# First FFN loop with shift rows from TensorE, and padded SBUF tiles: one layer of a latent diffusion backbone on Trainium2

## The chip, the core and the metric

The kernel runs on one NeuronCore of a Trainium2 chip. Its metric is the time of one execution in device microseconds (us). Three executions of the kernel before took 1124.28, 1126.04 and 1126.17 us; the median is 1126.04 us. Engines are named as in the profile: PE (TensorE, the matrix multiplier; PEld is its weight load), DVE (VectorE), ACT (ScalarE), POOL (GpSimd) and SP (SyncE, which issues nearly all DMAs here).

## What is computed

All of it is float32. `x` holds 512 latent tokens and `ctx` 256 context tokens, both 1024 wide. The change touches the first sublayer, for both streams:

```
mx = split(silu(c) @ w_ada + b_ada, 9)        # latent: shift, scale, gate, ...
mc = split(silu(c_ctx) @ w_ada + b_ada, 9)    # context
def ffn_sublayer(h_in, shift, scale, gate, norm_w, w1, w3, w2):
    h = rms_norm(h_in, norm_w) * (1 + scale) + shift
    return h_in + 0.5 * gate * swiglu(h, w1, w3, w2)
x   = ffn_sublayer(x,   mx[0], mx[1], mx[2], ...)    # D_FF = 2816
ctx = ffn_sublayer(ctx, mc[0], mc[1], mc[2], ...)
...   # token mixing (attention and gated MLP), then a second FFN, on x alone
```

## The kernel before, in words

Activations lie transposed: 128 features on the partitions, 8 such tiles (index `k`), 768 tokens on the free axis (two groups of 256 latent and 128 context columns). Each float32 product is made of three matmuls on operands that were split into a high part (rounded, type f32r) and a low part (the rest): high by high, high by low, low by high (`mm3`). Split weights lie in `oph`/`opl` tiles of 512 columns from a pool of 5 pairs (`ops`): ACT copies the high part, DVE subtracts for the low part. The FFN's input `h` lies split in `hh`/`hl`, its inner activation in `gh`/`gl`. A weight load takes 128 columns, 512 bytes of a partition.

**The first loop** begins the first FFN while its inputs still arrive. Before any feature tile `k` can be multiplied, the modulation of that tile must be known: a scale and a shift for each of 128 features and for both streams, each a dot product of 1024 elements with `silu(c)` or `silu(c_ctx)`. For the *scale*, PE multiplies the conditioning vectors (`scw`, 32 columns wide, two of them not zero) with the weights in eight small matmuls (`ada_row`, L330), ACT copies the row out (`ada_copy`), and one PE matmul against `sel` turns it into a column (`ada_col`, L340). For the *shift*, DVE multiplies a weight block laid out by output feature with the conditioning vector spread over all partitions (`cb`) and sums along the row: `ada_sum`, one instruction for each `k` and stream, 16 in all, tile `junk` in the profile. ACT then adds the bias (`ada_s`).

With both, `first_x` (DVE, tile `hfull`), `first_h` (ACT, tile `hh`) and `first_l` (DVE, tile `hl`) make tile `k` of `h`; `oph`/`opl` split the first-layer weights of tile `k` (tile `raw`, from `wfirst`). Then `step_mm(k)` (L604) runs twelve PE matmuls on 512 latent tokens, summed over `k` in four PSUM halves, and `first_ctx(k)` (L589) twelve on 256 context tokens. The loop is written out by hand, and its instructions keep their written order on each engine: step `k` opens with the column of tile `k+1` and the row of tile `k+2`, makes `h` of tile `k+1`, and multiplies tile `k`. The context's norm (squares by ACT, sums by DVE and one PE matmul) is made in steps 2 to 4, its `h` in steps 4 to 6, and `first_ctx` runs in pairs in steps 5 and 6 and for tiles 4 to 7 at the end.

After the loop come the rest of the first FFN, the mixing, and the second FFN, which a fast matrix scheme (tiles `t1h`, `b11h` and so on) runs on 256 columns.

Of the kernel before, what the change touches and what calls it, by code (L numbers as in the profile page):

```python
# [9 lines left out]
F32 = mybir.dt.float32  # L10
# [7 lines left out]
P = 128  # L18
# [155 lines left out]
def layer_kernel(ctx: ExitStack, tc: tile.TileContext, xT, wfirst, wst, wada, wuq, wkpe, cols, wrope, vnw, rope, out):  # L174
# [6 lines left out]
    opp = ctx.enter_context(tc.tile_pool(name="ops", bufs=1))  # L181
    st = Stream(nc, raws, opp, OPS, wst)
# [31 lines left out]
    accs = const.tile([P, NK, 2], F32, name="accs")  # L214
# [3 lines left out]
    b1n = const.tile([P, NK], F32, name="b1n")  # L218

# [15 lines left out]
    with right():  # L235
        hpool = hctx.enter_context(tc.tile_pool(name="hpool", bufs=1))
# [13 lines left out]
    scw = sp.tile([P, NK, 32], F32, bufs=1, name="sc")  # L250
    sc = scw[:, :, 0:2]
    sel = sp.tile([P, 2], F32, bufs=1, name="sel")
# [8 lines left out]
    sblk, units, raws_ = [], [], []  # L261

    def first_scale(k):
        ra = sp.tile([P, D], F32, tag="sa", bufs=3, name=f"scale_{k}")
        pin(nc.sync.dma_start(ra, wada[k][:, :D]))
        units.append([ra])

    def first_shift(k):
        if k % 2 == 0:
            pool, tag, bufs = (sp, "sb", 1) if k == 4 else (st.raw_pool, "block", BLOCKS)  # L270
            sblk.append(pool.tile([P, 2048], F32, tag=tag, bufs=bufs, name=f"shift_{k}"))
        rs_ = sblk[-1][:, (k % 2) * D : (k % 2) * D + D]
        pin(nc.sync.dma_start(rs_, wada[k][:, D:]))
        units[k].append(rs_)
# [6 lines left out]
    def first_units(k):  # L281
        first_scale(k)
        first_shift(k)
        first_raw(k)

    for k in range(3):
        first_units(k)
    nc.vector.tensor_reduce(sel, ident.rearrange("p (q c) -> p c q", c=32)[:, 0:2, :], axis=AX.X, op=ALU.add)
# [7 lines left out]
    def ada_dot(raw, c, which, to=None):  # L296
# [3 lines left out]
        nc.vector.scalar_tensor_tensor(  # L300
            out, raw, 1.0, cb[:, which, :], ALU.mult, ALU.mult,
            accum_out=acc[which][:, c : c + 1] if to is None else to,
        )
# [26 lines left out]
    def ada_row(d):  # L330
        for kt in range(NK):
            q = slice(kt % 4 * 32, kt % 4 * 32 + 32)
            pin(nc.tensor.matmul(pa[q, :P], scw[:, kt, :], units[d][0][:, kt * P : kt * P + P], start=kt < 4, stop=kt >= NK - 4))

    def ada_copy(d):
        row = sp.tile([P, P], F32, tag="row", name=f"row_{d}")
        nc.scalar.copy(row, pa[:, :P])
        return row

    def ada_col(row, d):  # L340
        o = pcol[:, 2 * d : 2 * d + 2]
        pin(nc.tensor.matmul(o, row, sel, start=True, stop=True))
        nc.scalar.activation(
            pairs[0][1][:, d, :], o, AF.Identity, bias=b1n[:, d : d + 1], scale=col[:, COL_N1 + d : COL_N1 + d + 1])
# [7 lines left out]
    def ada_shift(d, which):  # L352
        ada_sum(d, which)
        ada_s(d, which)
# [108 lines left out]
    def square1(j):  # L463
        sq = sp.tile([P, 512], F32, tag="sqx0", bufs=4, name=f"sq0_1{j}")
# [7 lines left out]
    def rstd_tiles(which):  # L472
        n = parts[which][1]
        return [sp.tile([P, n], F32, bufs=1, name=f"{s}{which}") for s in ("r0", "v")]
# [52 lines left out]
    put_cb(0)  # L527
    nc.vector.tensor_scalar_add(b1, col[:, COL_B : COL_B + 72], 1.0)
# [3 lines left out]
    def oph(k):  # L532
        ops[k] = st.pair() if k != OPS else [sp.tile([P, 512], F32R, tag="sqx0", bufs=4, name=f"op5{p}") for p in "hl"]
# [20 lines left out]
    put_cb(1)  # L554
    oph(0)
    steps(0)
    ada_row(0)
    row = ada_copy(0)
    late_sums(1)
    ada_col(row, 0)  # L560
    ada_sum(0, 0)
    ada_s(0, 0)
    root(1)
# [3 lines left out]
    first_units(3)  # L567
    ada_row(1)
    row = ada_copy(1)
    first_l(0, 0, 0)  # L570
    oph(1)
    steps(1)
    first_x(0, 0, 1)
    opl(1)
    first_h(0, 0, 1)
    first_units(4)
    load_x(0, 4, slice(256, 384))
# [35 lines left out]
    def step_open(k):  # L613
        ada_col(row, k + 1)
        if k + 2 < NK:
            ada_row(k + 2)

    sqs = []
    first_half(0)
    ada_col(row, 1)  # L620
    first_l(0, 0, 1)
    ada_row(2)
    row = ada_copy(2)
    ada_sum(1, 0)
    ada_s(1, 0)
    first_half(1)
    first_x(1, 0)
    first_h(1, 0)
    ada_sum(2, 0)
    first_l(1, 0)  # L630
    oph(2)
    opl(2)
    ada_s(2, 0)
    first_scale(5)
    load_x(4, 4, slice(256, 384))
    first_shift(5)
    first_raw(5)

    step_open(1)
    first_x(2, 0)  # L640
    first_h(2, 0)
    row = ada_copy(3)
    ada_sum(0, 1)
    first_l(2, 0)
    ada_sum(3, 0)
    oph(3)
    opl(3)
    ada_s(3, 0)
    ada_s(0, 1)
    step_mm(1)  # L650

    step_open(2)
    first_x(3, 0)
    first_h(3, 0)
    row = ada_copy(4)
    ada_sum(1, 1)
    oph(4)
    for j in (0, 1):
        sqs.append(square1(j))
    first_l(3, 0)  # L660
    ada_sum(4, 0)
    opl(4)
    ada_s(1, 1)
    ada_s(4, 0)
    step_mm(2)
    for k in (6, 7):
        first_scale(k)
        first_raw(k)
    for k in (6, 7):
        first_shift(k)  # L670

    step_open(3)
    first_x(4, 0)
    first_h(4, 0)
    for j in (2, 3):
        sqs.append(square1(j))
    row = ada_copy(5)
    ada_sum(5, 0)
    first_l(4, 0)
    ctx_add(2, 0)  # L680
    ctx_add(3, 1)
    ada_s(5, 0)
    oph(5)
    opl(5)
    ctx_add(2, 3)
    nc.vector.tensor_add(sqs[2][:, 0:256], sqs[2][:, 0:256], sqs[2][:, 256:512])
    step_mm(3)

    step_open(4)
    first_mm(4, 0)  # L690
    sumc = mm()
    sums(sumc, sqs[2][:, 0:256], True, True)
    first_mm(4, 1)
    first_x(5, 0)
    first_h(5, 0)
    row = ada_copy(6)
    first_l(5, 0)
    ada_sum(6, 0)
    ada_s(6, 0)
    rc = rstd_tiles(1)  # L700
# [4 lines left out]
    for j in (0, 1):  # L705
        first_x(j, 1)
        first_h(j, 1)
    ada_sum(2, 1)
    for j in (0, 1):
        first_l(j, 1)  # L710

    pcs += [mm() for _ in range(NFIRST)]
    step_open(5)
    first_x(6, 0)
    first_h(6, 0)
    row = ada_copy(7)
    ada_sum(3, 1)
    for j in (2, 3):
        ada_s(j, 1)
    first_l(6, 0)  # L720
    for j in (2, 3):
        first_x(j, 1)
        first_h(j, 1)
    ada_sum(7, 0)
    for j in (2, 3):
        first_l(j, 1)
    step_mm(5)
    for j in (0, 1):
        first_ctx(j)
    ada_s(7, 0)  # L730
    oph(6)
    opl(6)

    step_open(6)
    first_x(7, 0)
    first_h(7, 0)
    ada_sum(4, 1)
    first_l(7, 0)
    for j in (2, 3):
        first_ctx(j)  # L740
    oph(7)
    opl(7)
    ada_sum(5, 1)
    for j in (4, 5):
        ada_s(j, 1)
        first_x(j, 1)
        first_h(j, 1)
    ada_sum(6, 1)
    for j in (4, 5):
        first_l(j, 1)  # L750
    ada_sum(7, 1)
    for j in (6, 7):
        ada_s(j, 1)
        first_x(j, 1)
        first_h(j, 1)
    for j in (6, 7):
        first_l(j, 1)
    step_mm(6)

    step_mm(7)  # L760
    for j in range(4, NK):
        first_ctx(j)
# [1476 lines left out]
```

## Time and profile before

| | |
|---|---|
| median of three runs | 1126.04 us |
| the profiled execution | 1126.13 us |
| its span in the trace | 1124.3 us |
| PE busy | 1109.6 us, 99% of the span |
| DVE / ACT / POOL busy | 906.1 / 540.1 / 311.4 us |
| granted PE clock, mean | 0.998 |
| first loop, from the span's start to the first matmul of the next stage | 67.10 us |

Times in the trace count from the span's start; about 1.8 us of an execution lie outside the span. A matmul's recorded duration contains its pipeline's length, so that the records of neighbours overlap and busy PE time says little about its pace. The pace is the distance from one start to the next. A window of the trace counts every matmul that touches it, so (window + one recorded duration) / count gives that distance.

### The profile page before, as it was taken

To read this page: it belongs to the slowest core of one execution; us is meant where nothing else is said; L and a number is where in the kernel's file an instruction comes from. 1 tells how busy PE (TensorE), PEld (TensorE's weight loads), DVE (VectorE), ACT (ScalarE), POOL (GpSimd) and SP (SyncE) were. 2 spreads that over 40 slices of the span, in tenths; PEclk is the share of its full clock that TensorE was granted. 3 is DMA by queue.
4 is the path that set the end of the run, shared out by engine and by line. 5 is a ranking of instruction groups with operands and counts; after the bars stand their busy time and mean duration, and the time that the engine had idled before them with its cause. 6 is when DMAs were issued, how large, how long until landed. Compare 5 with 4: busy or idle time off the path is not lost.

```text
span 1124.3 us, 18769 instructions
## 1 busy us (share of the span) xinstructions
PE 1109.6 (99%) x7078; PEld 1060.7 (94%) x7078; DVE 906.1 (81%) x1669; ACT 540.1 (48%) x1119; POOL 311.4 (28%) x268
## 2 busy tenths in 40 slices
PE   8799999999999999999999999999999999999998
PEld 6699999999999999999998889999989989898997
DVE  7989999888888778866855899978886969686884
ACT  5555422441344213444755559985553535353451
POOL 0002402420343013300008427750014425162330
PEclk9999999999999999999999999999999999999999
DMA  9630253244234664322233211003221422233302
GB/s 350 215 113 20 102 194 121 96 164 151 94 131 150 230 207 167 129 66 87 85 131 93 76 38 35 25 20 116 73 95 57 148 79 84 105 113 113 114 1 94
DMA packets 35674, 125.89 MB, mean 112 GB/s; under 512 B 3712, under 2 KB 10624, under 8 KB 30976
## 3 DMA queue, kind: packets, MB, share of 16 engines
q1 hardware_dynamic: 35440, 124.63, 32.8%
q8 instruction: 56, 0.92, 0.3%
q14 instruction: 34, 0.28, 0.1%
q10 hardware_dynamic: 144, 0.06, 0.0%
HBM read 122.58 MB, written 2.10 MB: 111 GB/s over the span
## 4 chain that ended last, share of the span: by engine, by line
PE 91%; DVE 6%; ACT 1%; issue 1%; DMA 0%; POOL 0%; SPq 0%; DVEq 0%; POOLq 0%; ACTq 0%
PE mm L59 57%; PE one L59 20%; PE big L59 8%; PE mm L168 2%; PE mm L169 2%; PE mm L170 2%; DVE junk L59 1%; PE mm L589 1%; DVE opl L59 1%; DVE hfB L59 1%; DVE hfull L59 1%; DVE hl L59 1%; PE big L604 1%; DMA x<-xT 0%; DVE v L59 0%
## 5 line engine op out<-in xcount | busy, mean ns | idle before, releaser
L59 DVE TENSOR_TENSOR opl<-block,oph 128x512 fp32r<-128x512 f32 x216 | 192.3, 897 | 29.7 <-ACT oph L59 26.9
L59 POOL TENSOR_TENSOR block<-block 128x512 f32<-128x512 f32 x69 | 104.9, 1521 | 391.1 <-DVE opl L59 388.4
L59 ACT CAST oph<-block 128x512 fp32r<-128x512 f32 x216 | 133.8, 621 | 111.9 <-PE mm L59 85.1
L59 PE MATMUL mm<-gh,oph 128*128 128x384 f32 (+1 forms) x440 | 155.4, 353 | 0.0
L59 PE MATMUL mm<-gh,opl 128*128 128x384 f32 (+1 forms) x440 | 155.0, 352 | 0.0
L59 PE MATMUL mm<-gl,oph 128*128 128x384 f32 (+1 forms) x440 | 154.9, 352 | 0.0
L59 DVE SCALAR_TENSOR_TENSOR x<-mm,g,x 128x256 f32<-128x256 f32 (+2 forms) x184 | 84.6, 498 | 48.5 <-PE mm L59 48.2
L59 ACT CAST oph<-raw 128x512 fp32r<-128x512 f32 x115 | 69.9, 620 | 78.6 <-PE mm L59 53.1
L59 PEld LDWEIGHTS mm<-gh,opl 128*128 128x128 f32 x440 | 82.6, 188 | 5.7
L59 PEld LDWEIGHTS mm<-gl,oph 128*128 128x128 f32 x440 | 82.6, 188 | 5.6
L59 PEld LDWEIGHTS mm<-gh,oph 128*128 128x128 f32 x440 | 82.6, 188 | 5.6
L59 POOL TENSOR_TENSOR block<-s,block 128x512 f32<-128x512 f32 x35 | 48.0, 1371 | 143.7 <-DVE opl L59 143.1
L59 DVE TENSOR_TENSOR opl<-raw,oph 128x512 fp32r<-128x512 f32 x115 | 77.4, 688 | 7.2 <-ACT oph L59 6.5
L59 PE MATMUL mm<-hh,oph 128*128 128x384 f32 x192 | 64.9, 338 | 0.0
L59 PE MATMUL mm<-hh,opl 128*128 128x384 f32 x192 | 64.5, 336 | 0.0
L59 PE MATMUL mm<-hl,oph 128*128 128x384 f32 x192 | 64.5, 336 | 0.0
L59 DVE SCALAR_TENSOR_TENSOR junk<-raw,cb 128x1024 bf16<-128x1024 f32 x48 | 62.2, 1309 | 0.3 <-DMA raw<-wada 0.3
L59 POOL TENSOR_TENSOR s<-block 128x512 f32<-128x512 f32 x34 | 55.6, 1634 | 9.9 <-DMA block<-wst 9.9
L59 PE MATMUL one<-hh,opl 128*128 128x384 f32 x144 | 48.4, 336 | 0.0
L59 PE MATMUL one<-hh,oph 128*128 128x384 f32 x144 | 48.4, 336 | 0.0
L59 PE MATMUL one<-hl,oph 128*128 128x384 f32 x144 | 48.4, 336 | 0.0
L59 DVE SCALAR_TENSOR_TENSOR raw<-raw,cb 128x1024 f32<-128x1024 f32 x32 | 41.0, 1289 | 8.1 <-DMA raw<-wada 8.1
(685 smaller groups left out, 3403.0 us busy)
## 6 DMA issues: line engine op xcount, KB each, us to landing
raw<-wst SPq DMA_DIRECT2D x77, 512.0 KB, 3.9
block<-wst SPq DMA_DIRECT2D x36, 1024.0 KB, 4.9
raw<-wada SPq DMA_DIRECT2D x56, 512.0 KB, 4.3
scale<-wada SPq DMA_DIRECT2D x8, 512.0 KB, 8.4
shift<-wada SPq DMA_DIRECT2D x8, 512.0 KB, 8.9
x<-xT SPq DMA_DIRECT2D x5, 512.0 KB, 6.3
raw<-wfirst SPq DMA_DIRECT2D x8, 256.0 KB, 7.6
out<-x SPq DMA_DIRECT2D x7, 256.0 KB, 2.2
```

What stands on the lines that cost most here:

```text
L59: return lambda *a, **k: self.tc.keep_in_program_order(f(*a, **k))
L168: nc.tensor.matmul(out, lh, rh, start=first, stop=False, skip_group_check=more)
L169: nc.tensor.matmul(out, lh, rl, start=False, stop=False, skip_group_check=more)
L170: nc.tensor.matmul(out, ll, rh, start=False, stop=last, skip_group_check=more)
L589: pin(nc.tensor.matmul(o, l[:, c], r, start=k == 0 and m == 0 and w == 0, stop=k == NK - 1 and m == 2, skip_group_check=True))
L604: pin(nc.tensor.matmul(two(pbs[i]), l[:, c], lat(r, k), start=False, stop=k == NK - 1 and m == 2, skip_group_check=True))
```

## The change

**The first loop.** The shift's weights are laid out like the scale's, and PE makes both: `ada_row` runs 16 small matmuls in place of 8, the second eight with the conditioning vectors two columns further right in `scw` (now 34 columns wide), so that shift lands in its own two rows. `sel` has four columns, `ada_col` makes four values, and ACT finishes scale and shift with one instruction each. The 16 DVE dots, their 16 `ada_s` and the accumulators `accs` go. Scale and shift of a tile lie in one 1 MB tile (`scale_k`); four such tiles exist, two in the pool `block` and two in the pool `start`. All context work moves to the end: its columns of `x` are loaded after the last weights of `w_ada`, squares and sums stand in steps 5 and 6, and all eight `first_ctx` run behind `step_mm(7)`. The split weights of tiles 5, 6 and 7 lie in the pool `start`.

```diff
+    scw = sp.tile([P, NK, 34], F32, bufs=1, name="sc")
+    sc = scw[:, :, 2:4]
...
     def ada_row(d):
-        for kt in range(NK):
-            q = slice(kt % 4 * 32, kt % 4 * 32 + 32)
-            pin(nc.tensor.matmul(pa[q, :P], scw[:, kt, :], units[d][0][:, kt * P : kt * P + P], start=kt < 4, stop=kt >= NK - 4))
+        for w in range(2):
+            for kt in range(NK):
+                q = slice(kt % 4 * 32, kt % 4 * 32 + 32)
+                pin(nc.tensor.matmul(pa[q, :P], scw[:, kt, 2 - 2 * w : 34 - 2 * w], units[d][w][:, kt * P : kt * P + P],
+                                     start=w == 0 and kt < 4, stop=w == 1 and kt >= NK - 4))
...
     def ada_col(row, d):
...
+        nc.scalar.activation(pairs[0][0][:, d, :], o[:, 2:4], AF.Identity, bias=col[:, d : d + 1])
-    def ada_sum(d, which):
-        ada_dot(units[d][1], d, which, accs[:, d, which : which + 1])
-    def ada_s(d, which):
-        nc.scalar.activation(mod_s[0][which][:, d : d + 1], accs[:, d, which : which + 1], AF.Identity, bias=col[:, d : d + 1])
...
     step_mm(7)
-    for j in range(4, NK):
+    ctx_h((4, 5))
+    ctx_h((6, 7))
+    for j in range(NK):
         first_ctx(j)
```

On DVE, steps 3 and 4 of the loop before read as follows (`hfull`, `hl`: parts of `h`; `junk`: a shift's dot; `opl`, `op5l`: a low part of split weights; `sq`: the context's sum of squares):

```order
L59 SCALAR_TENSOR_TENSOR hfull<-x,a_79,v_214 128x2x256
L59 SCALAR_TENSOR_TENSOR junk_468,accs<-shift_279,cb 128x1024
L59 SCALAR_TENSOR_TENSOR hl<-hfull,s_78,hh 128x2x256
L59 TENSOR_TENSOR sq_12_461<-sq_12_461,sq_10_413 128x512
L59 TENSOR_TENSOR sq_13_463<-sq_13_463,sq_11_415 128x512
L59 TENSOR_TENSOR op5l<-raw_348,op5h 128x512
L59 TENSOR_TENSOR sq_12_461<-sq_12_461,sq_13_463 128x512
L59 TENSOR_TENSOR sq_12_461<-sq_12_461 128x256
L59 SCALAR_TENSOR_TENSOR hfull<-x,a_79,v_214 128x2x256
L59 SCALAR_TENSOR_TENSOR hl<-hfull,s_78,hh 128x2x256
L59 SCALAR_TENSOR_TENSOR junk_523,accs<-shift_446,cb 128x1024
```

And on DVE in the change, from step 4 to the context's norm:

```order
L59 SCALAR_TENSOR_TENSOR hfull<-x,a_83,v_224 128x2x256
L59 SCALAR_TENSOR_TENSOR hl<-hfull,s_82,hh 128x2x256
L59 TENSOR_TENSOR op6l<-raw_416,op6h 128x512
L59 SCALAR_TENSOR_TENSOR hfull<-x,a_83,v_224 128x2x256
L59 SCALAR_TENSOR_TENSOR hl<-hfull,s_82,hh 128x2x256
L59 TENSOR_TENSOR op7l<-raw_451,op7h 128x512
L59 TENSOR_TENSOR sq_11_575<-sq_11_575,sq_10_573 128x512
L59 TENSOR_TENSOR sq_12_577<-sq_12_577,sq_11_575 128x512
L59 TENSOR_TENSOR sq_13_579<-sq_13_579,sq_12_577 128x512
L59 TENSOR_TENSOR sq_13_579<-sq_13_579 128x256
L59 SCALAR_TENSOR_TENSOR hfull<-x,a_83,v_224 128x2x256
```

The dots are gone from between the parts of `h`, and the sums of squares stand behind the split of tile 7's weights, ahead of the last latent `hfull`.

On SP, the end of the loop's loads before (`scale`, `shift`: `w_ada`; `raw` from `wfirst`: first-layer weights; `x` in 128x8x128: context columns; `wst`: weights of the next stage):

```order
L258 DMA x_71<-xT 128x8x128
L265 DMA scale_5_343<-wada 128x1024
L258 DMA x_71<-xT 128x8x128
L273 DMA shift_4_279<-wada 128x1024
L278 DMA raw_347_348<-wfirst 128x512
L265 DMA scale_6_436<-wada 128x1024
L278 DMA raw_438_439<-wfirst 128x512
L265 DMA scale_7_441<-wada 128x1024
L278 DMA raw_443_444<-wfirst 128x512
L273 DMA shift_6_446<-wada 128x1024 x2
```

And in the change:

```order
L270 DMA scale_6_358<-wada 128x1024 x2
L274 DMA raw_367_368<-wfirst 128x512
L270 DMA scale_7_405<-wada 128x1024 x2
L274 DMA raw_415_416<-wfirst 128x512
L260 DMA x_75<-xT 128x8x128 x2
L127 DMA block_794_795<-wst 128x2048
L274 DMA raw_450_451<-wfirst 128x512
```

The context columns moved behind the last `scale` tile, and the last first-layer weights (`raw_450_451`, of tile 7) stand behind a 1 MB block of the next stage. Behind the loop the five engines' instructions stand in the same order as before.

**The padding.** Three unused tiles of 224, 256 and 32 bytes (per partition) shift what is allocated after them; `accs` (64 bytes) is gone.

```diff
+    ctx.enter_context(tc.tile_pool(name="pad2", bufs=1)).tile([P, 64], F32, name="pad_mid")
...
-    accs = const.tile([P, NK, 2], F32, name="accs")
...
+    const.tile([P, 56], F32, name="pad_left")
...
+        ctx.enter_context(tc.tile_pool(name="pad", bufs=1)).tile([P, 8], F32, name="pad_right")
```

The split weights move up by 224 - 64 = 160 bytes, the left side's tiles behind them (`gh`, `gl`) by 416, and the right side's tiles (`hh`, `hl`, and the second FFN's `t` and most `b` tiles, which grow downwards) go down by 32. In the built programs the tiles start at these bytes modulo 512: split weights at 416 before and 64 after, `gh`/`gl` at 416 and 320, `hh`/`hl` and the `t` tiles at 480 and 448. Slices of these tiles begin at multiples of 512 bytes, so a matmul's distance (start of the weights that are loaded under it less start of its moving operand, modulo 512) is the same for all slices. The counts below are of the built program's matmuls that stand beside one of the same width.

| columns | moving operand, weights | matmuls | distance before | after |
|---|---|---|---|---|
| 384 | `h` or its combinations `u`, split weights | 1750 | 448 | 128 |
| 384 | `g`, split weights | 983 | 0 | 256 |
| 512 | `g` or mixed heads, split weights | 601 | 0 | 256 |
| 512 | split weights, `h` as weights | 180 | 64 | 384 |
| 256 | `t`, `b` or `h`, split weights | 1832 | 448 | 128 |

The other f32r matmuls (attention, some 580 at distance 0 among them) keep their distance or are few.

More of the change, by code (lines that the diff above doesn't have):

```diff
@@ L279, in first_raw @@
         raws_.append(rw[:, :W1])
[L281 to L288, printed above, removed]
+    for k in range(4):
+        first_rows(k)
+        if k < 3:
+            first_raw(k)
+    nc.vector.tensor_reduce(sel, ident.rearrange("p (q c) -> p c q", c=32)[:, 0:4, :], axis=AX.X, op=ALU.add)
     warm = mm()
@@ L301, in ada_dot @@
             out, raw, 1.0, cb[:, which, :], ALU.mult, ALU.mult,
[L302 removed]
+            accum_out=acc[which][:, c : c + 1],
         )
@@ L473, in rstd_tiles @@
         n = parts[which][1]
-        return [sp.tile([P, n], F32, bufs=1, name=f"{s}{which}") for s in ("r0", "v")]
+        return [sp.tile([P, n], F32, bufs=1, name=f"{s}{which}") for s in (("v",) if which else ("r0", "v"))]
     def rstd_root(pt, r0):
@@ L566, in layer_kernel @@
     opl(0)
-    first_units(3)
-    ada_row(1)
+    root(1)
     row = ada_copy(1)
     first_l(0, 0, 0)
[L571 to L577, printed above, removed]
+    first_raw(3)
+    first_rows(4)
+    first_rows(5)
     pbs = bigs(4)
@@ L613, in step_open, with next_h @@
     def step_open(k):
-        ada_col(row, k + 1)
+        if k + 1 < NK:
+            ada_col(row, k + 1)
         if k + 2 < NK:
             ada_row(k + 2)
+    def next_h(k):
+        first_x(k, 0)
+        first_h(k, 0)
     sqs = []
     first_half(0)
+    oph(1)
     ada_col(row, 1)
+    steps(1)
+    first_x(0, 0, 1)
+    first_h(0, 0, 1)
+    next_h(1)
     first_l(0, 0, 1)
+    opl(1)
+    first_half(1)
     ada_row(2)
     row = ada_copy(2)
-    ada_sum(1, 0)
-    ada_s(1, 0)
-    first_half(1)
@@ L677, in layer_kernel @@
[L677 to L690, printed above, removed]
-    sumc = mm()
[L692 to L700, printed above, removed]
+    first_raw(6)
@@ new lines, in layer_kernel @@
+    for k in (0, 4):
+        load_x(k, 4, slice(256, 384))
+    for k in range(2, 5):
+        step_open(k)
+        next_h(k + 1)
+        row = ada_copy(k + 2)
+        first_l(k + 1, 0)
+        oph(k + 2)
+        opl(k + 2)
+        if k == 2:
+            first_raw(7)
+        step_mm(k)
+    step_open(5)
+    next_h(6)
+    row = ada_copy(7)
+    first_l(6, 0)
+    oph(7)
+    opl(7)
+    for j in range(4):
+        sqs.append(square1(j))
+    for a, b in ((1, 0), (2, 1), (3, 2)):
+        ctx_add(a, b)
```

161 lines of the change are left out of this document (43 added, 118 removed).

## The prediction

> **What bounds the kernel now.** First the page: busy time, and the chain of work that ended last.
>
> ```profile
> PE 1109.6 (99%) x7078; PEld 1060.7 (94%) x7078; DVE 906.1 (81%) x1669; ACT 540.1 (48%) x1119; POOL 311.4 (28%) x268
> PE 91%; DVE 6%; ACT 1%; issue 1%; DMA 0%; POOL 0%; SPq 0%; DVEq 0%; POOLq 0%; ACTq 0%
> ```
>
> PE holds 91% of the chain, DVE 6%. So two things can move the time: what keeps PE waiting in DVE's 6%, and the pace of the matmuls everywhere else. The change touches both, and I take them apart. The windows of the first loop and the end of its chain say where the 6% lies:
>
> ```profile
> core 0: us, PE busy (x) PEld busy (x) DVE busy (x) ACT busy (x) POOL busy (x), PEclk, DMA share, GB/s
> 0.00:16.50 16.50, 13.16 (x91) 10.39 (x91) 8.70 (x22) 10.89 (x22) 0.69 (x6) 1.00 0.92 326
> 16.50:40.00 23.50, 19.99 (x163) 15.17 (x164) 22.29 (x39) 12.60 (x33) 0.00 (x0) 1.00 1.03 374
> 40.00:51.40 11.40, 7.85 (x59) 6.22 (x58) 10.57 (x22) 5.94 (x15) 0.00 (x0) 1.00 0.20 58
> ...
> 55.72 5.70 PE big L604 x24
> 61.42 5.68 PE mm L589 x48
> 67.10 4.16 PE mm L59 x24
> ```
>
> DVE is busy 22.3 of 23.5 us and then 10.6 of 11.4, while PE has gaps; the loads are over at about 40 us (58 GB/s after it). From 51.4 us on PE runs without a wait and reaches the next stage at 67.10. DVE sets this loop, and after 40 us nothing else does.
>
> **The loop, step by step.** What goes from DVE is one row:
>
> ```profile
> L59 DVE SCALAR_TENSOR_TENSOR junk<-shift,cb x16: 1216/1218/1221, 14.1 to 59.4; 128x1024 bf16<-128x1024 f32 x16
> ```
>
> 16 x 1.22 us and their reads of the accumulator, some 20 us. DVE stops being the bound here, and the question is what is late next: PE's own work, or the loads. PE's work has these prices:
>
> ```profile
> 16.47 0.74 PE L596 MATMUL big<-hh,oph 128*128 128x256 f32 x4 [1.06 <-ACT hh L59]
> ...
> 20.41 0.63 PE L596 MATMUL big<-hh,opl 128*128 128x256 f32 x4
> ...
> 40.28 0.28 PE L342 MATMUL mm<-sel,row 128*128 128x2 f32 x2
> 40.49 0.65 PE L333 MATMUL mm<-scale,sc 128*32 128x128 f32 x16
> 41.06 0.73 PE L604 MATMUL big<-hh,op5h 128*128 128x512 f32 x2
> ```
>
> A column takes 0.21 us (40.28 to 40.49), a row 0.57 (to 41.06). The second eight matmuls follow with the pipeline full, so I price a double row at twice that less one start, 1.02 us; its bounds are 0.57 (all hidden) and 1.14. A step's twelve matmuls take 5.70 / 2 = 2.85 us, a context tile's 5.68 / 4 = 1.42. Both halves of tile 0 end at about 20.8 us (20.41 plus four matmuls); the steps ahead of that need the same loads and the same short DVE work, less one dot, plus a longer row while PE waits, so I leave 20.8. From there PE owes six double rows (6.1), six columns (1.3), seven steps (20.0), the context's sum (0.4) and eight context tiles (11.4): 39.2 us, and without a wait the next stage starts at **60.0 us**.
>
> The loads: 326 GB/s over 16.5 us and 374 over 23.5 is 14.2 MB by 40 us. In the order of the change, tile 7's first-layer weights come behind 2.1 MB of `x`, 8.4 of `w_ada`, 2.1 of `wfirst`, 1.0 of context columns and a 1.0 MB block of the next stage: 14.7 MB, so at 41.5 us. The wait is new: ACT's `oph` of tile 7 waits for it, and queued behind on ACT are the four squares and the last `hh`; behind these on DVE the sums of squares and the last `hfull`; PE's sum of the context, in the middle of step 6, waits for both. Rows of the loop before price them:
>
> ```profile
> 30.48 1.15 ACT L59 ACTIVATE sq<-x 128x512 f32<-128x512 f32 x2
> ...
> 37.17 0.68 DVE L59 TENSOR_TENSOR sq<-sq,sq 128x512 f32<-128x512 f32 x1
> 37.89 0.43 DVE L59 TENSOR_TENSOR sq<-sq 128x256 f32<-128x256 f32 x1
> ...
> 43.76 0.88 DVE L59 SCALAR_TENSOR_TENSOR hfull<-x,a,v 128x256 f32<-128x256 f32 x2
> ```
>
> The split of tile 7 takes 0.6 us, the squares 4 x 0.58, DVE's last two adds 1.1: the sum is ready at about 45.6. PE would reach it at 43.9. I add 1.7 us for that, 0.3 for tile 7's `h`, and 0.5 for short waits on ACT: **62.5 us**, or 4.6 us less than 67.10. The context's `h` (on DVE 16 x 0.44 us from 49 us on) stays ahead of its matmuls, 1.42 us a tile. The bounds: no wait, -7.1 us; or a longer wait that also costs the clock, as here after the gaps up to 51.4 us:
>
> ```profile
> 52.57 0.38 PE L589 MATMUL mm<-hl,oph 128*128 128x256 f32 x1
> ...
> 55.30 0.41 PE L589 MATMUL mm<-hh,opl 128*128 128x256 f32 x1
> ```
>
> 14 rows, so 13 spacings of 210 ns where 113 to 118 is usual: some 1.3 us lost, and that with 2 us more of waiting gives -1. Elsewhere DVE's relief is worth nothing, PE bounding.
>
> **The distances.** The loop is 6% of the time; the matmuls' pace is the rest. It is read from the first and last row of a stretch without a gap. In pairs: 384 columns at distance 448 (117 rows) and at 0 (118 rows), 256 columns at 448 (189) and at 0 (94), 512 columns at 0 (94) and at 64 (70).
>
> ```profile
> 83.75 0.34 PE L59 MATMUL big<-hl,oph 128*128 128x384 f32 x1
> ...
> 103.86 0.34 PE L59 MATMUL mm<-u2h,oph 128*128 128x384 f32 x1
> ...
> 149.69 0.33 PE L59 MATMUL mm<-gh,oph 128*128 128x384 f32 x1
> ...
> 169.97 0.33 PE L59 MATMUL mm<-gh,oph 128*128 128x384 f32 x1
> ...
> 857.79 0.28 PE L59 MATMUL one<-b21h,oph 128*128 128x256 f32 x1
> ...
> 879.93 0.28 PE L59 MATMUL one<-t2h,opl 128*128 128x256 f32 x1
> ...
> 754.78 0.28 PE L59 MATMUL mm<-mixh,uo1l 128*128 128x256 f32 x1
> ...
> 765.95 0.28 PE L59 MATMUL mm<-mixh,uo0l 128*128 128x256 f32 x1
> ...
> 895.84 0.39 PE L59 MATMUL mm<-gl,oph 128*128 128x512 f32 x1
> ...
> 916.94 0.39 PE L59 MATMUL mm<-gl,oph 128*128 128x512 f32 x1
> ...
> 612.88 0.40 PE L168 MATMUL mm<-oph,hh 128*128 128x512 f32 x1
> ...
> 628.99 0.40 PE L168 MATMUL mm<-oph,hh 128*128 128x512 f32 x1
> ```
>
> That gives 173.4 and 173.3 ns (20.11 / 116, 20.28 / 117); 117.8 and 120.1 (22.14 / 188, 11.17 / 93); 226.9 and 233.5 (21.10 / 93, 16.11 / 69). At distance 0, 128 more columns cost 53.2 and 53.6 ns, 0.417 a column, so pure streaming would be 106.8, 160.1 and 213.5 ns, and 13.3 ns of each matmul are something else. It does depend on the distance, but not in one direction: 448 is better than 0 at 256 columns and equal at 384; 64 is worse than 0 at 512. Nor on the distance alone:
>
> ```profile
> 46.46 0.28 PE L589 MATMUL mm<-hh,opl 128*128 128x256 f32 x1
> ...
> 48.84 0.28 PE L589 MATMUL mm<-hh,opl 128*128 128x256 f32 x1
> ...
> 64.11 0.28 PE L589 MATMUL mm<-hh,oph 128*128 128x256 f32 x1
> ...
> 65.64 0.28 PE L589 MATMUL mm<-hl,oph 128*128 128x256 f32 x1
> ```
>
> The same code at the same distance 448 runs at 113.3 ns (2.38 / 21) and then at 117.7 (1.53 / 13). The only rows of 384 columns at the distances 128 and 384 are those with `kpw` as weights, though its load is half as wide:
>
> ```profile
> L59 PE MATMUL mm<-hh,opl 128*128 128x384 f32 x192 | 64.5, 336 | 0.0
> L59 PE MATMUL mm<-hh,kpw 128*64 128x384 f32 x16 | 5.3, 332 | 0.0
> ```
>
> The recorded duration, 4 ns shorter, is the nearest row there is to the new distances. Class by class of the table in the section on the change:
>
> 384 columns, 2733 matmuls, to 128 and 256: between -4 ns (`kpw`) and +6.6 (what 64 costs against 0 at 512 columns). I take -2, half of `kpw`'s, for its load is half: **-5.5 us**; ends -10.9 and +18.0.
>
> 256 columns, 1832, to 128: between 113.3 and 120.1, so -4.5 and +2.3 ns. I take -2, between the two paces that one distance already shows: **-3.7 us**; ends -8.2 and +4.2.
>
> 512 columns, 601, from 0 to 256: between 0 and +6.6; I take +3, **+1.8 us**. And 180 from 64 to 384: between -6.6 and 0; I take -2, **-0.4 us**.
>
> Together -7.8 us. The Trainium skill speaks against all of it: "SBUF — State Buffer", section "Who interferes with whom", says that PE and ACT never wait on anyone, and "TensorE: Matmul & The Clock Gate", section on what happens when a matmul is issued, that loading the next weights takes no read bandwidth from the running matmul. By that rule the term is 0; the 117.8 against 120.1 ns above already disagree, though mildly. The latter page's section on the back-to-back gap gives N/2.4 + 2.5 ns, 162.5 at 384 columns; by it the most that distances could give, an estimate, would be some 50 us.
>
> **The sum.** 1126.13 (the profiled execution; 0.09 above the median) - 4.6 - 7.8 = 1113.7, so **1114 us**.
>
> **Rivals.** (a) *The distances do nothing*: matmul starts are set inside PE, and the small differences in the rows belong to their stages. For it: 448 and 0 are alike at 384 columns, and one distance shows two paces. Against: 120.1 at 0 beside 117.8 at 448, each over some 90 matmuls or more. Time: 1126.1 - 4.6 = 1121.5. That the loads eat the loop's gain as well (-1) is the same case's edge, 1125. (b) *The other 13 ns mostly go*: the weight load's reads meet the moving operand's and were at a bad distance everywhere. The best excess seen, 6.5 ns (113.3 - 106.8), for all: -6.8 x 2733 - 4.5 x 1832 - 6.9 x 601 = -31 us, so 1126.1 - 4.6 - 31 = 1090. (c) *The new distances are worse*: 384 columns at 128 and 256 behave as 512 columns do at 64, +6.6 ns. The price is +18 us at `hh` and `gh`, with 256 and 512 columns near zero: 1126.1 - 4.6 + 18 = 1139.5. It decides from +1.7 ns a matmul on (4.6 us / 2733), a quarter of the difference that 64 and 0 show. For it: 0 is the best distance on record at 512 columns, and 601 matmuls leave it.
>
> **How the numbers follow.** Forecast (1104 to 1119) 0.42; (a) 0.18, of which 0.04 is its edge; (b) or more 0.15; (c) 0.25, of which 0.03 stays within the bound. A measurement of this kernel tells about 0.2%, 2.3 us, from no change. Faster 0.42 + 0.14 + 0.15 = 0.71, same 0.04 + 0.03 = 0.07, slower 0.22. The range takes (a), most of (c) and (b) up to near its price: 1092 to 1136, with about 0.1 left out at each end.
>
> **What would show it.** The loop: no `junk` before the next stage, that stage starting at 60 to 64 us, and one PE wait of about 2 us for the context's sum; a start near 66 means that the loads or the clock took it. The distances: starts at 384 columns 171 ns apart, not 173.4; 256 columns 115 to 116; 512 columns near 230. 173.4 in both `hh` and `gh` is (a), under 168 is (b), over 175 is (c). The forecast is wrong if the classes move in opposite directions, for I took one mechanism for all, or if DVE, at 81%, becomes late once PE is faster.

## The result and the profile after

The changed kernel takes **1133.82 us** (median of four executions, 1132.93 to 1133.90) beside 1125.84 for the kernel before (four executions, 1124.28 to 1126.17): ratio 1.0076, 95% interval 1.0064 to 1.0088. It is 8 us slower; 12 us faster was forecast. The profiled execution took 1133.9 us, its span 1132.0, at a mean granted clock of 0.997. The page's busy times, and the engines' shares of the chain that ended last:

```profile
PE 1122.5 (99%) x7206; PEld 1074.6 (95%) x7206; DVE 889.6 (79%) x1637; ACT 537.7 (48%) x1111; POOL 307.8 (27%) x268
PE 95%; DMA 2%; ACT 1%; DVE 1%; issue 0%; POOL 0%; SPq 0%; DVEq 0%; POOLq 0%; ACTq 0%
```

DVE went from 6% of the chain to 1%, as the change meant it to. PE went from 91% to 95% and the loads (DMA) from 0% to 2%: most of what DVE gave up, PE took. Where in time it went is told by the point at which the next stage starts, in the chain's last steps of the first loop (start, duration, engine, tile, line):

```profile
47.26 1.19 PE mm L456 x2
...
54.92 11.44 PE mm L569 x96
66.36 4.22 PE mm L59 x24
```

The next stage starts at 66.36 us in place of 67.10. The loop has won 0.74 us, and the rest of the span has become longer: 1132.0 - 66.36 = 1065.6 against 1124.3 - 67.10 = 1057.2, **8.4 us**. From there on the engines' instructions stand in the same order in both kernels, PE bounding. So the pace is to be read, from first and last rows of stretches of PE's timeline in which no matmul waits. In pairs: 384 columns from `h` and `u`, at distance 128 (116 rows); 384 from `g`, at 256 (117); 256 columns, at 128 (169); 512 from `g`, at 256 (79).

```profile
84.67 0.34 PE L59 MATMUL big<-hh,oph 128*128 128x384 f32 x1
...
104.91 0.34 PE L59 MATMUL mm<-u3l,oph 128*128 128x384 f32 x1
...
149.74 0.33 PE L59 MATMUL mm<-gl,oph 128*128 128x384 f32 x1
...
169.85 0.33 PE L59 MATMUL mm<-gh,oph 128*128 128x384 f32 x1
...
869.78 0.28 PE L59 MATMUL one<-b22h,opl 128*128 128x256 f32 x1
...
889.94 0.28 PE L59 MATMUL one<-b22h,opl 128*128 128x256 f32 x1
...
904.76 0.39 PE L59 MATMUL mm<-gh,opl 128*128 128x512 f32 x1
...
922.44 0.39 PE L59 MATMUL mm<-gh,opl 128*128 128x512 f32 x1
```

That is 20.24 / 115 = **176.0 ns** where it was 173.4; 20.11 / 116 = 173.4 as before; 20.16 / 168 = **120.0** where it was 117.8; 17.68 / 78 = 226.7 as before (226.9). The recorded durations (0.34, 0.28 us to two digits) hardly show it. Two classes lost, and they are the two whose distance went from 448 to 128; the two that went from 0 to 256 stayed, and so did the small one that went from 64 to 384. Over all gapless stretches of the trace the means are 176.0 against 173.3 ns and 119.7 against 117.5: 2.7 x 1750 + 2.2 x 1832 = 8.8 us, the 8.4 us that the rest of the span lost.

The loop's 0.74 us in place of 4.6 has two further causes, both to be seen on the timelines. On ACT and DVE (`op7h`: the split of tile 7's weights; `sq`: the context's squares and sums; behind a row in brackets, how long the engine stood and what ended that):

```profile
42.66 0.62 ACT L59 CAST op7h<-raw 128x512 fp32r<-128x512 f32 x1 [2.06 <-DMA raw<-wfirst]
43.19 2.19 ACT L59 ACTIVATE sq<-x 128x512 f32<-128x512 f32 x4
44.37 2.28 DVE L59 TENSOR_TENSOR sq<-sq,sq 128x512 f32<-128x512 f32 x3 [0.36 <-ACT sq L59]
```

On PE, two 512-column matmuls to a row from 49.10 us on:

```profile
47.26 1.19 PE L456 MATMUL mm<-sq,ones 128*128 128x256 f32 x2 [3.23 <-DVE sq L59]
...
49.10 1.05 PE L584 MATMUL big<-hh,op6l 128*128 128x512 f32 x2
49.95 1.05 PE L584 MATMUL big<-hl,op6h 128*128 128x512 f32 x2
...
53.36 0.63 PE L584 MATMUL big<-hh,op7h 128*128 128x512 f32 x2
53.83 0.62 PE L584 MATMUL big<-hh,op7l 128*128 128x512 f32 x2
...
54.76 0.28 PE L569 MATMUL mm<-hh,oph 128*128 128x256 f32 x1
```

PE stands 3.23 us before the context's sum, which waits for the squares, which wait behind `op7h` for tile 7's weights, as the prediction had it. After that gap PE runs at half its pace: two matmuls take 0.85 us (49.10 to 49.95) until 53.36, then 0.47. The granted clock says the same (third number from the end of each row; columns as in the windows of the prediction):

```profile
40.00:51.40 11.40, 8.18 (x29) 6.33 (x28) 7.28 (x13) 6.51 (x14) 0.00 (x0) 0.79 0.66 259
46.50:53.40 6.90, 6.14 (x15) 4.84 (x16) 5.73 (x13) 3.85 (x7) 0.00 (x0) 0.51 0.13 52
51.40:67.10 15.70, 15.70 (x114) 14.95 (x113) 13.36 (x27) 8.66 (x19) 0.00 (x0) 0.94 0.22 66
```

### The profile page after: what moved, and what is told of

Same layout as the page of the kernel before. It is cut to its first block, busy times and chain, and to the rows that moved or that the text cites. A ratio compares the mean times of both kernels' runs of the same rounds, so it can differ in the third digit from the quotient of the medians.

```text
span 1132.0 us, 18985 instructions
## 1 busy us (share of the span) xinstructions
PE 1122.5 (99%) x7206; PEld 1074.6 (95%) x7206; DVE 889.6 (79%) x1637; ACT 537.7 (48%) x1111; POOL 307.8 (27%) x268
## 4 chain that ended last, share of the span: by engine, by line
PE 95%; DMA 2%; ACT 1%; DVE 1%; issue 0%; POOL 0%; SPq 0%; DVEq 0%; POOLq 0%; ACTq 0%
PE mm L59 56%; PE one L59 20%; PE big L59 8%; PE mm L168 2%; PE mm L169 2%; PE mm L170 2%; PE big L584 1%; PE mm L569 1%; DMA scale<-wada 1%; DMA raw<-wfirst 1%; PE big L170 1%; PE big L168 1%; PE big L169 1%; PE mm L327 1%; DMA x<-xT 0%
```

## The experiments

The theory after the result: the new distances cost 8.4 us in the two classes that went from 448 to 128, and the loop's own gain was eaten by the late load and the half clock. The rivals: the absolute place of the tiles matters, not the distance; or the loop's rewriting itself slows the later stages. Fifteen kernels were run, all timed beside the kernel before on the same chip. "Base" below is the kernel of which only the shown lines are changed.

### One half of the change at a time

loop_only is the changed kernel with the tiles of the kernel before in their places:

```diff
-    ctx.enter_context(tc.tile_pool(name="pad2", bufs=1)).tile([P, 64], F32, name="pad_mid")
...
-    const.tile([P, 56], F32, name="pad_left")
+    const.tile([P, 16], F32, name="pad_left")
...
-        ctx.enter_context(tc.tile_pool(name="pad", bufs=1)).tile([P, 8], F32, name="pad_right")
```

> The change's loop with every tile at the start it had before (split weights and g at 416, h at 480 modulo 512). Theory: the loop gives 0.7 us (next stage at 66.4 us in place of 67.1) and the distances cost the rest, so 1125.2, with starts 173.3 ns apart at 384 columns and 117.8 at 256. Rival: the loop itself puts the later stages into another rhythm; then 176.0 and 120.0 ns stay, and the time stays near 1134.

pads_only is the kernel before, with the three pads of the change (`pad_left` 40 floats, since `accs` is still there):

```diff
+    ctx.enter_context(tc.tile_pool(name="pad2", bufs=1)).tile([P, 64], F32, name="pad_mid")
...
+    const.tile([P, 40], F32, name="pad_left")
...
+        ctx.enter_context(tc.tile_pool(name="pad", bufs=1)).tile([P, 8], F32, name="pad_right")
```

> The loop of before with the change's starts (64, 320 and 448). Theory: 176.0 ns at 384 columns for h and u (1750 matmuls, +4.7 us), 173.3 for g, 120.0 at 256 columns (1832, +4.0 us), so 1134 to 1135. Rival (the loop made the rhythm): 173.3 and 117.8, and 1126.

Measured, beside 1124.54 us for the kernel before on this chip (15 executions): **pads_only 1132.84** (five, 1132.79 to 1134.73), ratio 1.0078, 95% interval 1.0066 to 1.0091; **loop_only 1124.46** (eleven, 1122.85 to 1125.59), ratio 0.9997, 0.9988 to 1.0006. The pads alone make the whole loss, and the loop alone gains nothing that could be measured. The pads' stretches of 384 (115 rows) and 256 columns (169 rows), with the old loop ahead of them:

```profile
84.81 0.34 PE L59 MATMUL big<-hh,opl 128*128 128x384 f32 x1
...
104.87 0.34 PE L59 MATMUL mm<-u3h,opl 128*128 128x384 f32 x1
...
869.74 0.28 PE L59 MATMUL mm<-t1l,oph 128*128 128x256 f32 x1
...
889.90 0.28 PE L59 MATMUL mm<-t1l,oph 128*128 128x256 f32 x1
```

20.06 / 114 = 176.0 and 20.16 / 168 = 120.0, the numbers of the changed kernel. In loop_only, on the other hand, PE's timeline and the chain's end read:

```profile
43.42 0.62 PE L582 MATMUL big<-hl,op6h 128*128 128x512 f32 x2
47.33 0.67 PE L454 MATMUL mm<-sq,ones 128*128 128x256 f32 x2 [3.29 <-DVE sq L59]
...
51.97 0.28 PE L567 MATMUL mm<-hh,oph 128*128 128x256 f32 x1
...
63.89 4.16 PE mm L59 x24
```

The same wait of 3.29 us, but in this execution no half clock: from the sum to the first context tile 4.64 us (47.33 to 51.97) against 7.50 in the changed kernel (47.26 to 54.76), and the next stage at 63.89. So the half clock cost the changed kernel's profile 2.9 us. It does not follow every such wait: loop_only's execution with this profile had a granted clock of 1.0 and took 1123.24 us, another at 1.0 took 1122.85, and the nine others, at 0.997 or 0.998, took 1124.26 to 1125.59.

### The late load

loop_raw7 has loop_only as its base; tile 7's weights get a tile of their own and are issued ahead of the context's columns and of the next stage's block.

```diff
-        rw = st.raw()
+        rw = gp.tile([P, W1], F32, tag="s1", bufs=4, name="raw7") if k == NK - 1 else st.raw()
...
     first_raw(6)
+    first_raw(7)
     for k in (0, 4):
...
-        if k == 2:
-            first_raw(7)
```

> As the first, but tile 7's first-layer weights have a tile of their own and are loaded ahead of the context columns and of the next stage's block. Theory: the wait of 6.8 us for that load and the half clock after it are what ate the loop's gain; without them the next stage starts at 60 to 62 us and the time is 1119 to 1121. Rival: PE's own added work or the context's chain is the bound; then the next stage starts at 65 us or later and the time is 1124 or more.

**1121.04 us** (five, 1120.72 to 1121.27), ratio to the kernel before 0.9967, 0.9954 to 0.9979; the granted clock was 1.0 in all executions. From the PE timeline and the chain:

```profile
45.40 0.67 PE L454 MATMUL mm<-sq,ones 128*128 128x256 f32 x2 [1.08 <-DVE sq L59]
...
61.96 4.16 PE mm L59 x24
```

The wait is 1.08 us in place of 3.29, the half clock is gone, and the next stage starts at 61.96, 5.1 us earlier than in the kernel before. The medians differ by 3.5 us only, because the execution of the kernel before that was profiled was one of its longer ones (1126.13 us, median 1124.54 here); the two profiled executions differ by 1126.13 - 1121.27 = 4.9 us. So the late load, with the half clock behind it, was what kept the loop's gain back. It is the base of what follows.

### Distance or place

shift_all is the kernel before with all three groups of tiles moved, and the distances kept (448 and 0): `pad_left` of 40 and `pad_right` of 88 floats, no `pad_mid`, so that the split weights and `g` start at 64 and `h`, `t` at 128 modulo 512.

> The kernel before with all three kinds of tiles at other starts (64, 64 and 128) but the distances of before (448 and 0). Theory (distance decides): 173.3 and 117.8 ns as before, 1126. Rival (a start's own place decides, a multiple of 64 where before it was 32 past one): 176 and 120 ns, 1134.

1124.32 us (one execution; the kernel before 1124.54). 172 gapless rows of 256 columns:

```profile
863.75 0.28 PE L59 MATMUL one<-b22h,oph 128*128 128x256 f32 x1
...
883.89 0.28 PE L59 MATMUL mm<-t1h,oph 128*128 128x256 f32 x1
```

20.14 / 171 = 117.8, as before the change. The place alone does nothing. dist_0_128 gives the two classes each other's distances, `h` and `t` 0 and `g` 128, and the next three put both at one distance:

```diff
+    ctx.enter_context(tc.tile_pool(name="pad2", bufs=1)).tile([P, 96], F32, name="pad_mid")
...
-    const.tile([P, 16], F32, name="pad_left")
+    const.tile([P, 32], F32, name="pad_left")
```

(`pad_mid` / `pad_left` in floats: dist_0_128 96 / 32, as shown; dist_64_64 112 / 48; dist_192_192 80 / 80; dist_320_320 48 / 112; below, dist_64_0 none / 48; dist_32_32 120 / 40; dist_480_480 8 / 24.)

> The last loop (early load for tile 7) with h at distance 0 and g at 128, the other way round than in the change. Theory (the distance decides, whatever the tile): g's 384 columns at 176.0 ns and h's at 173.3; h's 256 columns at 120.0; so 1121 + 2.7 x 0.98 + 2.5 x 1.8 = 1128. Rival (128 hurts only h, by something else in h's stages): g stays at 173.3.

> The same loop, h and g both at distance 64. Theory: each distance has a pace of its own for each width. Few rows show 64: 113 to 118 ns at 256 columns, 233 at 512; nothing at 384. If 64 mirrors 448 (the cost depends on how far apart the starts are, not on which is ahead), 173.3 and 117.5 ns, 1121. Rival (it depends on which is ahead): 64 lies towards 128, so 175 to 176 ns at 384 columns, some 1126 to 1128.

> h and g both at 192. Nothing on record is nearer than 128 (176.0 and 119.7 ns) and 256 (173.4 and 119.2). If the cost is a hump around 128, between them: 174 to 175 ns, 1124 to 1127. If 128 is the side of a larger hump, over 176 ns and over 1130.

> h and g both at 320. A few rows of attention at 256 columns show 113 to 118 ns there. If 256 to 448 is one flat stretch at 384 columns, 173.3 ns and 116 to 119 at 256 columns, 1120 to 1123. If some distance frees the matmul of the 13 ns, it is here or at 384: then below 170 ns and below 1112.

One execution each: 1129.33, 1124.32, 1122.06 and 1124.06 us (the kernel before on that chip, one execution: 1125.84). In dist_0_128 it is `g` that runs slowly at 384 columns (115 rows):

```profile
149.80 0.34 PE L59 MATMUL mm<-gh,oph 128*128 128x384 f32 x1
...
169.86 0.34 PE L59 MATMUL mm<-gh,oph 128*128 128x384 f32 x1
```

20.06 / 114 = 176.0, while `h` at 0 has 173.3. What is slow at 128 is whatever lies at 128. The other three fit none of their expectations: at 384 columns 64 gives 174.6 ns, between the two values that were expected; 192 gives 173.3, with nothing left of a hump around 128; and 320 gives 174.6, neither 173.3 nor below 170. The table gives the median of gapless groups of twelve matmuls (lowest to highest in brackets where they differ by over 3 ns), of these traces and of those before and after the change:

| distance | 256 columns | 384 columns | 512 columns, `g` moving | 512 columns, split weights moving |
|---|---|---|---|---|
| 0 | 120.0 | 173.3 | 226.7 (to 230.3) | 226.7 |
| 64 | 113.3 (to 117.8) | 174.6 | 233.3 | 233.3 |
| 128 | 120.0 | 175.8 | 232.5 | - |
| 192 | 117.8 (from 113.3) | 173.3 | 228.9 | 228.9 |
| 256 | 120.0 | 173.3 | 226.7 (to 230.3) | - |
| 320 | 113.3 (to 117.8) | 174.6 | 233.3 | 233.3 |
| 384 | - | - | - | 233.3 |
| 448 | 117.8 (from 113.3) | 173.3 | - | 228.9 |

The pattern repeats every 256 bytes (0 and 256, 64 and 320, 192 and 448 agree in every column that has both), and what is best at one width is not at another: 64 is the best distance for 256 columns and the worst for 512.

### Best distance, and the theory's fall

If the distance sets the spacing, then 64 for the second FFN's 256 columns, and nothing else moved (but `b12`, from 0 to 320), should win. ffn2_64 does that on the base loop_raw7:

```diff
+        hactx.enter_context(tc.tile_pool(name="pad3", bufs=1)).tile([P, 32], F32, name="pad_ffn2")
         hap = hactx.enter_context(tc.tile_pool(name="hap", bufs=1))
...
+    t4.tile([P, 48], F32, bufs=1, name="pad_b12")
     B12 = block(t4, "b12")
```

> The loop of loop_raw7; all tiles of the first FFN where they were before; only the second FFN's 256-column t and b tiles are moved, from distance 448 to 64 (and b12 from 0 to 320). If the table of spacings by distance and width holds for single tiles, 1,647 matmuls of 256 columns drop from about 117.6 to 114.5 ns (-5.1 us) and 48 from 120.0 to 114.5 (-0.3), while the 384-column matmuls stay at 173.3 and 173.4: loop_raw7's 1121.04 becomes 1115.6 (1115 to 1116.5). If the 114 ns of the runs at distance 64 and 320 came from the first FFN's tiles too (the split weights' or the g tiles' own starts), the spacing stays near 117.6 and the time near 1121.

> The loop of loop_raw7, h/u and t/b at distance 64, g at 0. By the table: 256 columns 114.5 (1,788 x -3.1 = -5.5 us), 384 columns from h and u 174.7 (1,750 x +1.4 = +2.5), from g 173.4 and 512 from g 226.9 (unchanged), split weights moving against h weights at 448, near 229 (180 x -4.2 = -0.8): 1121.0 - 3.8 = 1117.2. If what a class does depends on the other class's distance as well, the g or the h numbers leave these.

> The loop of loop_raw7, h and g both at distance 32, halfway between two points of the table. If the spacing varies smoothly with the distance, each class lies between its values at 0 and 64: 256 columns about 117.2, 384 about 174, 512 from g about 230, and the time near 1122. If only steps of 64 bytes count (32 acts as 0), 256 columns 120.0, 384 173.4, 512 226.9: +2.4 x 1,830 = 4.4 us, 1125.4. If 32 bytes off a multiple of 64 costs by itself, all classes lie above both neighbours.

> The loop of loop_raw7, h and g both at distance 480, which the period of 256 makes 224, halfway between 192 and 256. Smooth: 256 columns about 118.8, 384 173.4, 512 from g about 228; time near 1123. Steps of 64 (as 448): 117.6, 173.3, 229.0, near 1122 as with both at 192. A cost of 32 bytes by itself: all above 120.0, 173.4 and 229.

**ffn2_64 took 1120.29 us** (five, 1120.20 to 1120.71; the kernel before 1125.86 on this chip, nine executions; ratio 0.9953, 0.9940 to 0.9967) where 1115.6 was expected; dist_64_0 1121.43 where 1117.2 was; dist_32_32 1125.92, dist_480_480 1123.63 (one execution each). In ffn2_64, 172 rows at distance 64:

```profile
863.84 0.28 PE L59 MATMUL mm<-t2h,oph 128*128 128x256 f32 x1
...
883.98 0.28 PE L59 MATMUL mm<-t2h,oph 128*128 128x256 f32 x1
```

117.8 ns (20.14 / 171), not 113.3. The theory that the distance alone sets the spacing falls with that. In dist_64_64, where 113.3 came from, two stretches of the second FFN at the same distance, with 179 and with 66 rows, read:

```profile
857.73 0.28 PE L59 MATMUL one<-b21h,opl 128*128 128x256 f32 x1
...
877.90 0.28 PE L59 MATMUL one<-t2h,oph 128*128 128x256 f32 x1
...
883.73 0.28 PE L59 MATMUL one<-b22h,oph 128*128 128x256 f32 x1
...
891.38 0.28 PE L59 MATMUL mm<-t4h,opl 128*128 128x256 f32 x1
```

20.17 / 178 = 113.3 and 7.65 / 65 = 117.7: **two paces at one distance**, each kept through a stretch, with a short wait of PE between them. At 64, 192, 320 and 448 stretches of 256 columns run at one or the other; at 0 and 128 none of the traces has 113.3. The other widths are not free of it: `h` at distance 64 has 173.3 ns in dist_64_0 and 174.6 in dist_64_64. The two finer steps fit none of their expectations at all widths: at 32 bytes the spacings are 118.3, 173.3 and 233.3 ns (256, 384, 512 columns), at 480 they are 116.7, 173.3 and 233.3. At 256 columns both lie between the values at the neighbouring steps, and at 512 both are as slow as the slowest distance.

### What picks the pace

The two theories left: something in the addresses beyond the distance, or only the instant at which a stretch begins. relock_448 (base loop_raw7) and relock_64 (base ffn2_64) change no address. They put one extra matmul ahead of each unit of the second FFN but the first, of 16, 32, 48 and so on up to 256 columns, into the output that the next matmul (`start=True`) writes over:

```diff
+            if self.n == 256 and blk == "T1" and RELOCK:
+                w = RELOCK.pop(0)
+                if w:
+                    nc.tensor.matmul(bank[:, :w], a[0][:, :P], self.blocks[blk][0][:, 0, :w], start=True, stop=False, skip_group_check=True)
             prod(bank, a, self.blocks[blk], self.n, first)
```

> loop_raw7 (second FFN's t and b tiles at distance 448), with one extra matmul ahead of the T1 product of each Winograd unit but the first of the second FFN, of 16, 32, 48 ... 256 columns and once 64; its output is written over by the matmul behind it, so nothing that is computed changes. If the instant at which a stretch begins picks its pace, some of the 17 widths leave the unit's following 84 matmuls at 113.3 ns and others at 117.8, a mixture where loop_raw7 has 117.8 in all; each unit that changes gains 84 x 4.5 = 0.38 us against 0.1 to 0.2 us for its extra matmul: total 1119 to 1123. If addresses beyond the distance pick it, all units stay at 117.8 and the 17 extra matmuls cost 2 us: 1123.

> ffn2_64 (second FFN's t and b tiles at distance 64), with the same 17 extra matmuls. If the instant picks the pace, units of 113.3 and of 117.8 ns, set by the width, and if the two distances work alike, by the same widths as in relock_448; 1118 to 1122. If not, 117.8 throughout and about 1122.3.

1121.54 and 1120.52 us (one execution each), and both have units of either pace. In relock_448, behind the extra matmul of 16 columns (72 rows from 851.80) and behind that of 32 (at 859.96; 70 rows from 861.72):

```profile
851.80 0.28 PE L60 MATMUL one<-b21h,oph 128*128 128x256 f32 x1
...
859.85 0.28 PE L60 MATMUL one<-b22h,opl 128*128 128x256 f32 x1
859.96 0.39 PE L60 MATMUL mm<-t1h,oph 128*128 128x32 f32 x2
...
861.72 0.28 PE L60 MATMUL mm<-b21h,opl 128*128 128x256 f32 x1
...
869.85 0.28 PE L60 MATMUL mm<-b22h,opl 128*128 128x256 f32 x1
```

8.05 / 71 = 113.4 and then 8.13 / 69 = 117.8, with the same tiles at distance 448. There 16 and 144 columns give the fast pace, both directly behind 512-column matmuls, where 80, 208 and 240 do not; in relock_64 it is 32, 80, 112, 176, 192 and 224. So the start of a stretch picks the pace, with no address changed. That it is the instant fits the widths; and at distance 64 other widths are good than at 448. relock_16 uses this: loop_raw7 with 16 columns at the five places where 512-column matmuls give way to 256-column ones.

```diff
+RELOCK_W = [0, 16, 0, 0, 0, 16, 0, 0, 0, 16, 0, 0, 0, 16, 0, 16]
```

> loop_raw7 (second FFN's t and b tiles at distance 448 as before) with an extra matmul of 16 columns at five places only: where 512-column matmuls of a down projection give way to the 256-column ones of the second FFN; the matmul behind it writes its output over. If the start picks the pace and it holds, the five gapless stretches (336 three times, 168, 216, 1,392 matmuls) run at 113.3 in place of 117.8: -6.3 us, +0.6 for the five extra matmuls; 1121.0 becomes about 1115.4, up to 1117.5 where PE then waits for the weight splits, as in the run with both distances at 64. If the pace falls back within a stretch or the starts pick it by chance, 1118 to 1122.

**1118.15 us** (five, 1117.97 to 1118.44; the kernel before 1124.50, eight executions), ratio 0.9942, 0.9928 to 0.9956: the fastest of all, though 1115.4 was expected. Its timeline has 179 rows, then the end of that stretch, then 74 rows:

```profile
851.75 0.28 PE L60 MATMUL one<-t1l,oph 128*128 128x256 f32 x1
...
871.92 0.28 PE L60 MATMUL one<-b21h,opl 128*128 128x256 f32 x1
...
878.04 0.28 PE L60 MATMUL one<-t4h,opl 128*128 128x256 f32 x1
878.35 0.39 PE L60 MATMUL one<-b22h,oph 128*128 128x256 f32 x1
878.57 0.28 PE L60 MATMUL one<-b22l,oph 128*128 128x256 f32 x1
...
878.81 0.28 PE L60 MATMUL one<-b22h,oph 128*128 128x256 f32 x1
...
887.40 0.28 PE L60 MATMUL mm<-t4l,oph 128*128 128x256 f32 x1
```

20.17 / 178 = 113.3 up to 878.04; then two spacings are 0.31 and 0.22 us, and the stretch goes on at 8.59 / 73 = 117.7. The waits of that place name the releaser, an addition of DVE (waited for: us in total, times, longest):

```profile
PEld one L60 <- DVE u L60: 0.2, 1, 0.2
```

The gain is what could be kept: 1,129 matmuls of the trace run at 113.3 in place of 117.8 (5.1 us), six such stops cost 1.5 and the five extra matmuls 0.55 (228 ns for the pair that takes the place of one of 118), together 3.0; measured, 1121.04 - 1118.15 = 2.9 (on two chips, where the kernel before takes 1124.54 and 1124.50).

## Why the prediction was wrong

**What bounds the kernel** was right. DVE left the chain (6% to 1%), and in its place stand loads: `scale` at the start, with 8.79 us of the chain, and later the one that was named.

**The loop, -4.6 us forecast, -0.74 in the changed kernel's profile, nothing measurable in loop_only's time.** The mechanism was right: the one PE wait that came is for the context's sum, behind tile 7's weights, and PE came to it at 47.26 - 3.23 = 44.0 us, where 43.9 was worked out. Its terms were mis-sized. The weights were there at 42.66 (forecast 41.5): SP issued their load at 35.88, having stood 3.0 us until PE had read the buffer that the next stage's block takes, and it landed 6.76 us later. The sum began at 47.26 (45.6), +1.7 us. The half clock after the gap, +2.9, stood in the bounds with 1.3 and not in the sum. The matmuls up to the first context tile took 0.9 less than the 5.5 allowed for them, and the 96 context matmuls, at the new distance, 0.2 more: 62.5 + 1.7 + 2.9 - 0.9 + 0.2 = 66.4. With the load moved forward on SP the next stage started at 61.96 us in loop_raw7. That this is near the forecast 62.5 does not confirm it, for 62.5 was worked out with the load in its late place; there, without the half clock, loop_only's profile has 63.89.

**The distances, -7.8 us forecast, +8.4 measured: the step that failed.** It is the sentence for 384 columns, "I take -2, half of `kpw`'s", and its sister for 256 columns; what the runs put in their place is +2.7 ns x 1750, 0 x 983, +2.2 ns x 1832, 0 x 601 and 0 x 180 (233.3 at 64 and at 384). The nearest row was no guide. The changed kernel's row for the same matmuls:

```profile
L59 PE MATMUL mm<-hh,kpw x16: 333/336/339, 551.1 to 575.5; 128*64 128x384 f32 x16
```

They keep their distances, 128 and 384, in both kernels, and take 336 ns after the change and 332 before it. So the 332 did not belong to the distance at which they stood. The better row was on record too: `h` at 448 was as good as the best seen at 384 columns, and one of the two good paces at 256, so the classes that gave it up had little to win by what the rows showed; of the bounds, -4 and +6.6 ns, the upper one rested on a full-width row.

The two paces of one distance, 113.3 and 117.7 ns, were shown in the prediction and used as bounds. They were the key: relock_448 and relock_64 show that the start of a stretch, with no address changed, chooses between them. Since 0 and 256 act as one distance (the table), two of the five classes' terms were 0 for a reason that the traces of before could not show.

**The rivals.** (c), the new distances are worse, is what happened, with 2.7 and 2.2 ns on 3,582 matmuls in place of 6.6 ns on 2,733; its point of decision, 4.6 us, was passed. (a) falls with pads_only: distances do something, 8.3 us. The rule that the prediction quotes from the Trainium skill ("SBUF — State Buffer", "Who interferes with whom"), that PE never waits on anyone, does not cover where PE's own operands lie: 120.0 against 117.8 and 176.0 against 173.4 ns, with nothing moved but addresses. (b) falls with the table: no distance has a median under 113.3, 173.3 and 226.7 ns. Of the signs named, "over 175 is (c)" was met by `h` (176.0) and not by `g` (173.4): the classes did not move together, which the prediction had given as what would make it wrong. Its last warning, that DVE becomes late once PE is faster, came true where the 256 columns of the second FFN took the fast pace: PE waits there for DVE's addition into `u` in relock_16, dist_64_64, dist_320_320 and relock_64, and not in loop_raw7 or the kernel before.

What stays open is the cause inside the chip. That the weight load's reads meet the moving operand's fits a period in bytes and a choice by the instant of the start, but no run here shows the reads. And at distance 128, where the changed kernel stands, no start was varied. Its 256-column groups are not all alike either: from 792 to 836 us, 17 of them run at 118.2 to 119.2 ns in place of 120.0. Whether a start could give 113.3 there is not shown.

## What to carry to other kernels

Take the spacing of matmuls from starts, never from recorded durations, and stretch by stretch: a mean over a class hid two paces here. A few hundred unused bytes ahead of the other tiles cost this kernel 0.8%, so after any change of the allocation compare spacings class by class before judging the change itself; loop and pads were two changes here, and the useful one was not seen behind the other. And a load that is moved behind a block of the next stage is worth a look at its landing before anything that waits for it is counted as a gain.

## What had not been expected of the hardware

- With f32r operands, the spacing of matmuls depends on the distance between the weights being loaded and the moving operand, with a period of 256 bytes, by up to 6.6 ns at 512 columns and 2.5 at 384 (medians in the table above), and differently at each width. At 256 columns the medians run from 113.3 to 120.0, but there the distance does not decide alone.
- At the same addresses 256-column matmuls hold one of two paces, 113.3 or 117.8 ns, over hundreds of matmuls (distances 64, 192, 320 and 448). One matmul of 16 columns at the start of a stretch, or a wait of 0.2 to 0.3 us within it, can change from one to the other.
- Half clock followed waits of PE well under 3.4 us, and it did not follow every such wait. A gap of 3.23 us was followed by about 6 us at half pace in the changed kernel's profile (47.26 to 53.36) and one of 3.29 us by none in loop_only's; a gap of 1.08 us was followed by none in loop_raw7. But in the kernel before, two gaps of 0.87 and 0.95 us between 49.20 and 52.60 us were followed by a granted clock of 0.50 from 52.60 to 56.00, and in pads_only one of 1.41 us by 0.50 from 36.40 to 39.80. The Trainium skill ("TensorE: Matmul & The Clock Gate", the part on the clock gate) has a free-running window of some 3.4 us, and half clock after an idle window. That like gaps end differently agrees with a window that runs freely; that the window must be idle throughout does not agree with these gaps, which are all shorter.
